# One encoder layer on one core: the order of its stages changed, and seven-product multiplication used for 102 pairs of tiles instead of 81

## The chip, the core and the metric

The kernel runs on one core of one Trainium2 chip, in one launch. The metric is device time in microseconds (us). Times are the median of three runs of the kernel before, 1941.53 us, between 1939.39 and 1941.59. The profile comes from one further execution, which took 1940.43 us.

## What is computed

One layer of a bidirectional encoder: 256 tokens, width 4096, all in float32. The parts that matter here:

```python
h = rms_norm(x, g_mix)
proj = h @ w_in                                   # 4096 -> 1600 + 2048 + 4 x 2048
c_q, c_kv, k_rope, gate_a, q_b, k_b, v_b, gate_b = split(proj)   # 1024, 512, 64, then 2048 each
# latent heads (16): small projections of the latent columns, then dense softmax attention
q_a = rms_norm(c_q) @ w_uq                        # 1024 -> 16 x (128 + 64), the 64 rotated by position
kv  = rms_norm(c_kv) @ w_ukv                      # 512 -> 16 x (128 + 128)
y_a = rms_norm(attention(q_a, kv, k_rope)) * silu(gate_a)
# dilated heads (16): attention with a distance penalty over three window patterns
y_b = rms_norm(dilated(q_b, k_b, v_b)) * silu(gate_b)
x = x + concat(y_a, y_b) @ w_out                  # 4096 -> 4096
gate = sigmoid(rms_norm(x, g_ple) @ w_ple_gate)   # 4096 -> 4096
out = rms_norm(x + (p @ w_ple) * gate, g_final)
```

## The kernel before

**A product.** Every float32 operand of a large multiplication is cut into a high half (rounded by ACT) and a low half (the remainder, by DVE); `split` does it. `mm` then issues three matmuls: high by high, high by low, low by high. The left operand is the transposed activation, kept as tiles of 128 contraction rows by 256 tokens; the right operand is a weight tile of 128 rows by up to 1024 columns, loaded by DMA on SP's queue into one of four `raw` buffers and cut into halves shortly before its use.

**Steps.** All multiplications by weights are laid out in one list, `steps`, in the order in which TensorE takes them. Two kinds of groups fill the list. A `Chunk` takes up to 512 columns in two PSUM banks, two contraction tiles in one step. A `Block` takes 1024 columns in eight banks: its plain steps multiply one contraction tile with four products (two halves of the tokens by two halves of the columns), twelve matmuls of 512 columns. Its fast steps take a *pair* of contraction tiles as a 2 x 2 by 2 x 2 multiplication with seven products in place of eight. For that they need four differences of weight tiles (`fast_steps`, on DVE) whose high and low halves are made anew, and sums and differences of the left operand, which `add_sums` makes once for a stage and several blocks use. The last products are put together on DVE from the banks M1 to M7, M2, M3, M4 and X, in a `mid` task after the last fast step and a `done` task after the block's last step. `spread(n, lead, trail)` lays n pairs between `lead` and `trail` plain steps.

**Tasks.** What is not a weight multiplication (attention of a head, turning a tile, gating, statistics) is a Python generator. `advance` resumes it when a model of the engines' clocks says that its inputs are due no later than `SOON` = 0.3 us after TensorE is free; what the task then emits stands at this place in the queue of each engine. Before, `advance` runs after each step of the list. Weight tiles are converted ahead of their step (`convert_one`), two to five steps.

**The order before.** With the pairs of each block in brackets:

1. latent columns of `w_in` in four chunks of 400, while x is loaded, turned and squared (`x_bank`, `x_square`);
2. a block of latent gate columns (6);
3. eight times: projections `w_uq` and `w_ukv` of two latent heads, between them 512 gate columns (`ga2`), and the attention of the heads (`attend` with `dil` false); then a last gate chunk `ga3`;
4. blocks for the dilated q, k, v, 1024 columns each, in the order q, k, v, q, k, v (6, 8, 8, 8, 8, 4);
5. dilated gate columns in four chunks of 512, 64 steps, beside the attention of the dilated heads;
6. `w_out` in three blocks (4, 7, 4) and two chunks;
7. `w_ple_gate` in three blocks (6 each) and chunks of 512, 256 and 256 columns, with `w_ple`; then the final norm.

All vector, scalar and matmul instructions are recorded at one line of the helper that meters them, L174 (L176 in the changed kernel), so groups are told apart by tiles. The tile names in the profile are `hi` and `lo` for halves of weights, `raw` for loaded weights, `A`, `B`, `T`, `Q` for the large SBUF buffers, and `m`, `s`, `o`, `t` for PSUM banks.

Of the kernel before, what the change touches and what calls it, by code (L numbers as in the profile page):

```python
# [66 lines left out]
class Clock:  # L67
# [31 lines left out]
    def after(self, ap, engine, wrote):  # L99
        name, lo, hi = self.place(ap)  # L100
        times = [self.base.get(name, 0.0)]
        for m in self.marks.get(name, ()):
            if m[0] < hi and lo < m[1]:
                for who in m[2:3] if wrote else m[2:]:
                    times += [t for e, t in who.items() if e != engine]
        return max(times)
# [12 lines left out]
    def run(self, engine, us, outs, ins, late=0.0):  # L119
        at = self.free[engine]  # L120
        for ap in ins:
            at = max(at, self.after(ap, engine, True))
        for ap in outs:
            at = max(at, self.after(ap, engine, False))
        self.free[engine] = at + us
        if late:
            self.free["dma"] = max(self.free["dma"], at + 2.0) + late
            seen = self.free["dma"]
        else:
            seen = at + us + self.SEEN[engine]  # L130
# [65 lines left out]
class Chunk:  # L196
# [4 lines left out]
    def __init__(self, src, nk, n, lhs, banks, done, needs=lambda j: (), per=2, ts=(0, 1), keep=None):  # L201
        self.src, self.nk, self.n, self.lhs, self.banks = src, nk, n, lhs, banks
        self.done, self.needs, self.per, self.ts, self.keep = done, needs, per, ts, keep
        self.ps, self.ring = None, WP
# [3 lines left out]
def encoder_layer(ctx: ExitStack, tc: tile.TileContext, x, p, positions, g_mix, w_in, g_q_latent, w_uq,  # L208
# [61 lines left out]
    nc.gpsimd.dma_start(gains[:32, 0, :], g_mix[0].rearrange("(k p) -> k p", p=P))  # L270
# [37 lines left out]
    def rotary_tables():  # L308
# [26 lines left out]
        nc.scalar.activation(ss[:, :, :half], ss[:, :, half:], AF.Copy, scale=-1.0)  # L335

# [89 lines left out]
    def advance(force=False, spare=True):  # L426
# [21 lines left out]

    def load_x(i):
        xs[i] = slot(f"T{i % 4}", [NT, 512])  # L450
        for o in (0, 256) if i == 0 else (0,):
            n = 256 if i == 0 else 512
# [11 lines left out]
    def x_square(b):  # L464

        i, o = divmod(b, 2)
        if o:
            nc.scalar.activation(xjunk[:, 0], xs[i][:, o], AF.Square, accum_out=sq[:, o, i:i + 1])
        else:
            nc.vector.scalar_tensor_tensor(xjunk[:, 1], xs[i][:, o], 1.0, xs[i][:, o], op0=ALU.mult, op1=ALU.mult,  # L470
                                           accum_out=sq[:, o, i:i + 1])

    def x_bank(b):
# [5 lines left out]
        x_square(b)  # L479

    rx, rxq, rxh = stat(NT), stat(NT), stat(NT)

    def x_stats():
# [4 lines left out]
        nc.vector.tensor_scalar(rxh, rx, 0.5, None, op0=ALU.mult)  # L488

# [4 lines left out]
    c_tok = []  # L494
# [5 lines left out]

    def turn_c(bs):

        for b in bs:
            tag = yield from turned()
            tp = bank(tag, [2, S])
            for k in range(2):
                for t in range(NT):
                    nc.tensor.transpose(tp[:, k, t * P:(t + 1) * P], c_tok[t][:, (2 * b + k) * P:(2 * b + k + 1) * P],
                                        ident)
            yield  # L510
            key, o = ("q", 2 * b) if b < 4 else ("kv", 2 * b - 8)
            split_rows(*(q[:, o:o + 2] for q in cT[key]), tp, G[key][:, o:o + 2])
            give(tag)
            yield

    def done_a(i):
        def task(ps):
            if i == 0:
                yield from x_stats()
                for t in range(NT):  # L520
                    c_tok.append(slot(f"B{t}", [OFF_GA]))
                qh, ql = slot("B4", [8, S], F32R), slot("B5", [8, S], F32R)
                kv = slot("B6", [2, 4, S], F32R)
                cT["q"], cT["kv"] = (qh, ql), (kv[:, 0], kv[:, 1])
            for t in range(NT):
                dst = c_tok[t][:, 400 * i:400 * (i + 1)]
                if t:
                    nc.vector.tensor_scalar(dst, ps[t], rx[:, t:t + 1], None, op0=ALU.mult)
                else:
                    nc.scalar.activation(dst, ps[t], AF.Copy, scale=rx[:, t:t + 1])  # L530
            give(*ps.tags)
            yield
            if i == 3:
                spawn(latents())
            ends = [400 * i, min(400 * (i + 1), Q_LORA + KV_LORA)]
            if ends[0] < Q_LORA < ends[1]:
                ends.insert(1, Q_LORA)
            for lo, hi in zip(ends, ends[1:]):
                c = 4 if lo == Q_LORA else 5 if lo > Q_LORA else i
                for t in range(NT):  # L540
                    nc.scalar.activation(junk[:, :hi - lo], c_tok[t][:, lo:hi], AF.Square,
                                         accum_out=sums[:, c, t:t + 1])
                    yield
            while i and ("cT", i - 1) not in flags:
                yield
            yield from turn_c(((0,), (1, 2), (3,), (4, 5))[i])
            flags.add(("cT", i))
            if i == 3:
                tot = stat(2 * NT).rearrange("p (a t) -> p a t", a=2)
                nc.vector.tensor_tensor(tot[:, 0], sums[:, 0], sums[:, 1], op=ALU.add)  # L550
                nc.vector.tensor_tensor(tot[:, 0], tot[:, 0], sums[:, 2], op=ALU.add)
                nc.vector.tensor_tensor(tot[:, 1], sums[:, 4], sums[:, 5], op=ALU.add)
                yield from rsqrt_mean(rq, tot[:, 0], Q_LORA)
                nc.vector.tensor_scalar(rqs, rq, (NOPE + ROPE) ** -0.5, None, op0=ALU.mult)
                yield from rsqrt_mean(rkv, tot[:, 1], KV_LORA)
                flags.add("latents")
        return task

    def latents():
        kpe = slot("T6", [2, NT, 2, ROPE])  # L560
        for t in range(NT):
            for d in range(2):
                nc.gpsimd.tensor_copy(kpe[:, 1, t, d], c_tok[t][:, Q_LORA + KV_LORA:OFF_GA])
        rk = slot("T5", [NT, 2, ROPE])
        rotate(rk, kpe[:, 1], kpe[:, 0], 2)
        pe = slot("T7", [4, S], F32R)
        T7["pe"] = pe
        yield
        tag = yield from turned()
        tp = bank(tag, [2, S])  # L570
        for t in range(NT):
            nc.tensor.transpose(tp[:, 0, t * P:(t + 1) * P], rk[:, t].rearrange("p d r -> p (d r)"), ident)
        yield
        split(pe[:, 0], pe[:, 1], tp[:, 0])
        give(tag)
        flags.add("kpe")
# [3 lines left out]
    E = {}  # L580

    def attend(h, q_src, k_src, pe, v, y, dil):
# [18 lines left out]
        at_s, at_o = ("m0", "m1") if dil else ("s", "o")  # L601
# [86 lines left out]
    def done_uq(i):  # L688
        def task(ps):
            q = slot("T5", [NT, 2, NOPE + ROPE])  # L690
            kq = slot("T6", [1024])
# [16 lines left out]
            while i and not all(("scored", 0, 2 * i - 1 - n) in flags for n in range(2)):  # L708
                yield
            pe = slot("Q0", [2, S], F32R)  # L710
# [7 lines left out]
    def done_uk(i):  # L718
        def task(ps):
            if i == 0:  # L720
                E["t"] = slot("T4", [2, NT, S])
                E["s"] = stat(2 * 3 * NT).rearrange("p (i a t) -> p i a t", i=2, a=3)
                for j in range(2):
                    ya[j] = slot(f"B{2 + j}", [8, S])
            pr = pairs[i]
            k = pr["kq"][:, :512].rearrange("p (t h d) -> p t h d", t=NT, h=2)
            v = slot(f"B{i % 2}", [2, NT, 2, HD], F32R)
# [1074 lines left out]
```

## Time and profile before

| | before |
|---|---|
| median of 3 runs | 1941.53 us (1939.39 to 1941.59) |
| profiled execution | 1940.43 us, span 1938.7 us |
| TensorE busy, matmuls | 1914.6 us (99%), 9290 |
| weight loads | 1630.6 us (84%) |
| VectorE busy | 1540.0 us (79%) |
| ScalarE busy | 1093.8 us (56%) |
| DMA | 370.59 MB, mean 191 GB/s |

The page gives busy time by engine, the span in 40 slices, the DMA queues, the chain of work that ended last and the costliest groups of instructions. In a row of a group stand the instruction with its output and inputs, shapes and count, then busy time and mean duration of one in ns, then the idle time of the engine before these instructions and what ended it. In the table of stretches each row has the window in us, then for each engine the busy time and, in brackets, the number of instructions.

### The profile page before, as it was taken

Reading aid. Unit: us, or ns where it says so; the run is one execution under the profiler, and the core shown is the slowest. Engines: PE = TensorE matmul, PEld = TensorE weight load, DVE = VectorE, ACT = ScalarE, POOL = GpSimd, SP = SyncE. Lnnn points to the kernel's source line nnn. Section 1 sums busy time; section 2 is a strip of 40 time slices with the busy share of each in tenths; the row PEclk is TensorE's granted clock in tenths of the full one; section 3 lists DMA queues with packets and bytes.
Section 4 is the critical chain, followed back from the end, with each engine's and each line's share of the span. In section 5 each row is a group of like instructions: output and inputs, shape, how many; then the busy total and the mean of one; then the engine's idle time right before and its main releaser. Section 6 shows DMA issues by size and latency. Waiting matters only on the chain.

```text
span 1938.7 us, 25562 instructions
## 1 busy us (share of the span) xinstructions
PE 1914.6 (99%) x9290; PEld 1630.6 (84%) x9290; DVE 1540.0 (79%) x2131; ACT 1093.8 (56%) x1500; POOL 81.2 (4%) x124
## 2 busy tenths in 40 slices
PE   9999999999999999999999999999999999999997
PEld 8998889887788888888888888788888888888887
DVE  7846966666999999999677778889976688889765
ACT  6644555655565565656446666555654456555543
POOL 1001012220000000000000110000000000000000
PEclk9999999999999999999999999999999999999998
DMA  7666644445666666666754456665666656666665
GB/s 252 195 189 194 199 147 152 140 148 159 185 200 207 211 201 196 211 203 207 218 176 142 141 163 194 229 212 182 215 196 202 187 184 215 196 215 194 230 183 176
DMA packets 146478, 370.59 MB, mean 191 GB/s; under 512 B 11924, under 2 KB 45808, under 8 KB 146096
## 3 DMA queue, kind: packets, MB, share of 16 engines
q1 hardware_dynamic: 144432, 361.80, 60.7%
q0 software_dynamic: 1920, 7.15, 1.1%
q8 instruction: 73, 1.20, 0.2%
q14 instruction: 53, 0.43, 0.1%
HBM read 364.72 MB, written 4.19 MB: 190 GB/s over the span
## 4 chain that ended last, share of the span: by engine, by line
PE 89%; DVE 6%; DMA 2%; ACT 2%; issue 1%; DVEq 0%; ACTq 0%; POOLq 0%
PE m L174 51%; PE t L174 17%; PE s L174 11%; PE o L174 10%; DVE lo L174 2%; DVE B L174 1%; DVE T L174 1%; DMA raw<-in_w_ple_gate_dram 1%; ACT hi L174 1%; DMA raw<-in_w_out_dram 1%; DVE Al L174 1%; DMA raw_e<-in_w_ple_dram 0%; DVE st L174 0%; DVE Ah L174 0%; ACT B L174 0%
## 5 line engine op out<-in xcount | busy, mean ns | idle before, releaser
L174 DVE TENSOR_TENSOR lo<-raw,hi 128x1024 fp32r<-128x1024 f32 (+4 forms) x501 | 559.1, 1125 | 240.8 <-ACT hi L174 239.9
L174 ACT ACTIVATE hi<-raw 128x1024 fp32r<-128x1024 f32 (+4 forms) x501 | 488.6, 981 | 423.4 <-PE m L174 146.8
L174 PE MATMUL m<-hi,Ah 128*128 128x512 f32 (+2 forms) x711 | 265.3, 373 | 1.8 <-DVE B L174 1.0
L174 PE MATMUL m<-hi,B 128*128 128x512 f32 (+1 forms) x838 | 265.6, 376 | 0.1
L174 PE MATMUL m<-hi,Al 128*128 128x512 f32 (+2 forms) x717 | 264.0, 368 | 0.0
L174 PE MATMUL m<-lo,Ah 128*128 128x512 f32 (+2 forms) x708 | 261.3, 369 | 1.3 <-DVE lo L174 1.3
L174 DVE TENSOR_TENSOR B<-raw,B 128x1024 fp32r<-128x1024 f32 (+2 forms) x238 | 210.8, 911 | 21.0 <-ACT B L174 18.5
L174 ACT ACTIVATE B<-raw 128x1024 fp32r<-128x1024 f32 (+1 forms) x126 | 121.4, 970 | 99.8 <-PE m L174 24.9
L174 PEld LDWEIGHTS m<-hi,B 128*128 128x128 f32 x838 | 156.0, 188 | 22.6 <-DVE B L174 0.5
L174 PE MATMUL m<-lo,B 128*128 128x512 f32 (+1 forms) x419 | 157.2, 375 | 3.8 <-DVE lo L174 3.8
L174 PEld LDWEIGHTS m<-hi,Ah 128*128 128x128 f32 x711 | 134.2, 189 | 20.1 <-issue 1.7
L174 PEld LDWEIGHTS m<-hi,Al 128*128 128x128 f32 x717 | 135.1, 188 | 18.2 <-DVE Al L174 0.2
L174 PEld LDWEIGHTS m<-lo,Ah 128*128 128x128 f32 x708 | 133.5, 189 | 19.6 <-DVE lo L174 3.0
L174 PE MATMUL m<-B,Ah 128*128 128x512 f32 (+1 forms) x440 | 127.9, 375 | 0.8 <-DVE B L174 0.8
L174 PE MATMUL t<-hi,Al 128*128 128x512 f32 x250 | 97.2, 390 | 0.0
L174 PE MATMUL t<-hi,Ah 128*128 128x512 f32 x246 | 97.1, 395 | 0.0
L174 ACT ACTIVATE hi<-B 128x1024 fp32r<-128x1024 f32 x74 | 77.6, 1059 | 30.3 <-PE t L174 9.8
L174 PEld LDWEIGHTS m<-B,Ah 128*128 128x128 f32 x440 | 80.4, 188 | 16.1 <-DVE B L174 0.9
L174 PE MATMUL t<-lo,Ah 128*128 128x512 f32 x240 | 93.6, 390 | 0.0
L174 PEld LDWEIGHTS m<-lo,B 128*128 128x128 f32 x419 | 78.8, 188 | 17.6 <-DVE lo L174 6.9
L174 DVE TENSOR_TENSOR lo<-B,hi 128x1024 fp32r<-128x1024 f32 x74 | 88.4, 1219 | 5.6 <-ACT hi L174 4.9
L174 PE MATMUL m<-B,Al 128*128 128x512 f32 (+1 forms) x220 | 82.2, 374 | 0.0
(488 smaller groups left out, 3679.1 us busy)
## 6 DMA issues: line engine op xcount, KB each, us to landing
raw<-in_w_in_dram SPq DMA_DIRECT2D x320, 512.0 KB, 4.2
raw<-in_w_out_dram SPq DMA_DIRECT2D x128, 512.0 KB, 4.5
raw<-in_w_ple_gate_dram SPq DMA_DIRECT2D x128, 512.0 KB, 4.6
raw<-in_w_in_dram SPq DMA_DIRECT2D x63, 400.0 KB, 3.5
raw<-in_w_uq_dram SPq DMA_DIRECT2D x32, 384.0 KB, 3.4
raw<-in_w_ukv_dram SPq DMA_DIRECT2D x16, 512.0 KB, 5.0
T<-in_x_dram SPq DMA_DIRECT2D x7, 512.0 KB, 5.8
T<-in_x_dram POOLq DMA_DIRECT2D x7, 512.0 KB, 5.9
```

Source lines behind the costliest of these rows:

```text
L174: return do(out, *rest, **named)
```

## The change

The list of steps is laid out in another order, again with the pairs of each block:

1. the six q, k, v blocks first (3, 7, 7, 8, 8, 6); the first of them begins with contraction tiles 16 to 31, since x now arrives in that order, and one product order differs in its first step;
2. latent columns in chunks of 384, 384, 384 and 448, beside the attention of the dilated heads;
3. all gate columns as four blocks, dilated then latent (5, 7, 7, 7);
4. `w_uq` and `w_ukv` of the eight pairs of latent heads with no other columns between them, uq in banks m0 and m1, ukv in m2 and m3;
5. `w_out` with the rows of the dilated heads first: for columns 3072 to 4095 as two half chunks (`half_o` adds them to the residual), then three blocks over all rows (6, 6, 4), then the other half chunks;
6. `w_ple_gate` in three blocks (7 each) and the same last chunks.

That is 102 pairs. Buffers are given out anew to fit. `advance` is now also called after every product (`tick`), with a second condition, `room() > ROOM`, for resuming a task. The clock model keeps one DMA queue per issuing engine and orders reads and writes of one engine differently. Some tasks change the engine or the order of an operation: `x_square` squares on ACT alone, `done_a` squares out of PSUM, `done_uk` interleaves its two token tiles, and the last stage reads half of the embedding product out of PSUM instead of a copy.

```diff
-        self.free = dict.fromkeys([*self.SEEN, "dma"], 0.0)
+        self.free = dict.fromkeys(self.SEEN, 0.0)
...
-                if due.get(task, 0.0) <= clock.free["pe"] + SOON and (spare or force or task not in lazy):
+                if due.get(task, 0.0) <= clock.free["pe"] + SOON and (force or (spare or task not in lazy) and room() > ROOM):
                     resume(pool, task)
...
+    X_ORDER = 4, 5, 6, 7, 0, 1, 2, 3
...
-        if o:
-            nc.scalar.activation(xjunk[:, 0], xs[i][:, o], AF.Square, accum_out=sq[:, o, i:i + 1])
-        else:
-            nc.vector.scalar_tensor_tensor(xjunk[:, 1], xs[i][:, o], 1.0, xs[i][:, o], op0=ALU.mult, op1=ALU.mult,
-                                           accum_out=sq[:, o, i:i + 1])
+        nc.scalar.activation(xjunk[:, o], xs[i][:, o], AF.Square, accum_out=sq[:, o, i:i + 1])
...
+    C_COLS = (0, 384), (384, 384), (768, 384), (1152, 448)
...
             self.left[m] -= 1
             mm(self.ps[m], a, b, first, self.left[m] == 0)
+            tick()
...
+            more = [*needs, *self.turn_needs]
...
-                self.step("M5 M7", None, lambda hi, lo: split(hi, lo, T[0]), run(("M5", S(0)), ("M7", S(2))), needs, 0, 1.37),
-                self.step("M6 M4", None, lambda hi, lo: split(hi, lo, T[1]), run(("M6", S(1)), ("M4", A22)), needs, 0, 1.37),
+                self.step("M5 M7", None, lambda hi, lo: split(hi, lo, T[0]), run(("M5", S(0)), ("M7", S(2))), more, 0, 1.37),
+                self.step("M6 M4", None, lambda hi, lo: split(hi, lo, T[1]), run(("M6", S(1)), ("M4", A22)), more, 0, 1.37),
...
-    FAST, WIDE = 6, 3
+    FAST, WIDE = 7, 3
...
+    FAST_QKV, LEAD_QKV = (3, 7, 7, 8, 8, 6), (18, 4, 4, 4, 4, 8)
+    FAST_G, LEAD_G = (5, 7, 7, 7), (12, 6, 6, 4)
+    FAST_O, LEAD_O = (6, 6, 4), (4, 5, 4)
...
+    for i, (lo, n) in enumerate(C_COLS):
+        add(Chunk(cols(w_in, lo, n), 32, n, lhs_x, (("m2", "m3"), ("m0", "m1"))[i % 2], done_a(i)))
...
+    for n, (dil, half) in enumerate(((1, 0), (1, 1), (0, 0), (0, 1))):
+        hook(len(steps), only(*(("t0", "t1"), ("m2", "m3"))[n % 2]))
+        order = spread(FAST_G[n], LEAD_G[n], 4)
...
+        blk.turn_needs = ["latents", *(("gated", 1, c) for c in range(min(4, 2 * n)))]
...
+    for i in range(8):
+        for ch in (Chunk(cols(w_uq, 384 * i, 384), 8, 384, lhs_c("q"), ("m0", "m1"), done_uq(i), lambda j: ["latents"]),
+                   Chunk(cols(w_ukv, 512 * i, 512), 4, 512, lhs_c("kv"), ("m2", "m3"), done_uk(i),
...
+    def room():
+
+        c, now = converted[0], ran[0] + 1
+        if c >= len(steps):
+            return 1e9
+        need = max(clock.free["pe"], step_end[0]) + sum(steps[k].time for k in range(now + 1, c))
+        return need - max(clock.free[e] for e in ("dve", "act", "pe"))
+
+    def tick():
+
+        advance(spare=slack(ran[0] + 1) > MARGIN)
```

More of the change, by code (lines that the diff above doesn't have):

```diff
@@ L512, in turn_c @@
-            split_rows(*(q[:, o:o + 2] for q in cT[key]), tp, G[key][:, o:o + 2])
+            split(pe[:, 0], pe[:, 1], tp[:, 0])
             give(tag)
[L514 to L556, printed above, removed]
-        return task
@@ L559, in latents @@
[L559 to L576, printed above, removed]
+            flags.add("latents")
@@ L1521, in encoder_layer @@
[L1521 to L1534 removed]
+            opening = blk
@@ L1629, in split @@
                 return
-            r = raw.pop(i)
-            for k in range(ch.per) if i == 0 else (slice(None),):
-                if i == 0:
-                    split(*lhs_x(k), first[k], G["mix"][:, k:k + 1])
-                split(hi[:, k], lo[:, k], r[:, k])
+            split(hi, lo, raw.pop(i))
             if ch.keep:
```

515 lines of the change are left out of this document (291 added, 224 removed).

## The prediction

> **What bounds the kernel now.** I read the page first, then the table of stretches, then PE's waits, then the groups by shape, last single instructions in time order.
>
> ```profile
> span 1938.7 us, 25562 instructions
> PE 1914.6 (99%) x9290; PEld 1630.6 (84%) x9290; DVE 1540.0 (79%) x2131; ACT 1093.8 (56%) x1500; POOL 81.2 (4%) x124
> PEclk9999999999999999999999999999999999999998
> PE 89%; DVE 6%; DMA 2%; ACT 2%; issue 1%; DVEq 0%; ACTq 0%; POOLq 0%
> ```
>
> TensorE holds 99% of the span and 89% of the chain that ended last, at full clock. VectorE is next at 79%. A busy PE row is modelled, so the rate of issue has to confirm it:
>
> ```profile
> 100.00:150.00 50.00, 50.00 (x280) 49.95 (x279) 24.25 (x26) 22.36 (x34) 0.00 (x0) 1.00 0.70 191
> 300.00:350.00 50.00, 49.33 (x286) 44.53 (x285) 31.61 (x48) 28.96 (x56) 10.77 (x18) 1.00 0.46 142
> 550.00:600.00 50.00, 50.00 (x223) 41.39 (x222) 48.67 (x58) 28.16 (x30) 0.00 (x0) 1.00 0.67 219
> 700.00:750.00 50.00, 50.00 (x222) 41.41 (x221) 48.85 (x56) 30.23 (x32) 0.00 (x0) 1.00 0.69 221
> 850.00:900.00 50.00, 50.00 (x222) 41.42 (x221) 49.33 (x59) 31.47 (x34) 0.00 (x0) 1.00 0.67 206
> 1050.00:1100.00 50.00, 50.00 (x271) 42.73 (x270) 41.67 (x73) 37.59 (x72) 5.85 (x5) 1.00 0.50 146
> ```
>
> The columns are PE, weight loads, DVE, ACT, POOL with their counts, clock, DMA share and GB/s. In stages of 512-column matmuls 222 go through in every 50 us, 0.2252 us each, whatever the other engines do; with 400 columns it is 50/280 = 0.1786 us. The same 222 at three places says that these stages are PE's own pace. The row of 850 us also says that DVE may be busy for 49.33 of 50 us without one lost matmul. What PE waits for by name is little, and half of it lies in the stage of the latent heads (250 to 500 us):
>
> ```profile
> PE m L174 <- DVE lo L174: 5.1, 13, 0.8
> PE m L174 <- DVE B L174: 1.8, 4, 0.7
> PE m L174 <- DVE junk L174: 1.5, 1, 1.5
> PE t L174 <- DVE B L174: 1.1, 1, 1.1
> ...
> PE m L174 <- DVE lo L174: 3.1, 8, 0.8
> PE t L174 <- DVE B L174: 1.1, 1, 1.1
> PE m L174 <- DVE B L174: 0.7, 1, 0.7
> ```
>
> The first four rows are the whole span, the last three the window 250 to 500 us: 4.9 us there. The kernel is bound by the number of matmuls; what can spoil a cut in that number is a DVE without room, or heads whose steps PE has to wait for.
>
> A rule of the Trainium skill (Perfetto Trace Analysis, Identifying the Most-Contended Engine) would have headroom read from the share of weight loads, not of matmuls. By the 84% above TensorE would have a sixth to spare, and fewer matmuls would bring less than their count. The trace does not bear that out: in the rows with 222 matmuls the loads are busy 41.4 of 50 us too, and no matmul is lost there.
>
> **The change part by part.** *Fewer products.* A pair of contraction tiles multiplied in the seven-product form needs seven products instead of eight, and a product is three matmuls of 512 columns. 21 pairs more are 63 matmuls fewer; the order of the two programs' instructions agrees (6762 matmuls of 512 columns before, 6699 after). All pairs lie in the stages of 0.2252 us: 63 x 0.2252 = **-14.2 us**.
>
> The latent columns are cut as 384, 384, 384 and 448 instead of four times 400:
>
> ```profile
> 297.19 0.51 PE L174 MATMUL m<-hi,B 128*128 128x384 f32 x2
> 297.54 0.33 PE L174 MATMUL m<-lo,B 128*128 128x384 f32 x1
> 297.71 0.51 PE L174 MATMUL m<-hi,B 128*128 128x384 f32 x2
> ```
>
> Three of 384 columns take 297.71 - 297.19 = 0.52 us, 0.173 each; 448 lie between 0.1786 and 0.2252, 0.199. Before: 768 x 0.1786 = 137.2 us; after: 576 x 0.173 + 192 x 0.199 = 137.9. No difference beyond the rounding: **0**. Transposes and attention matmuls keep their counts.
>
> A second rule speaks against part of this. The Trainium skill (TensorE: Matmul & The Clock Gate, Back-to-back issue gap) gives about 131 ns for a sustained matmul of 512 columns. By it 63 would bring 8.3 us only. Here a sustained one takes 225 ns in every such stretch.
>
> *What a pair costs DVE and ACT.*
>
> ```profile
> L174 DVE TENSOR_TENSOR lo<-raw,hi 128x1024 fp32r<-128x1024 f32 x365 | 443.8, 1224 | 199.1 <-ACT hi L174 198.2
> L174 DVE TENSOR_TENSOR lo<-B,hi 128x1024 fp32r<-128x1024 f32 x74 | 88.4, 1219 | 5.6 <-ACT hi L174 4.9
> L174 DVE TENSOR_TENSOR B<-raw,B 128x512 f32<-128x512 f32 x112 | 77.0, 688 | 1.9
> L174 DVE TENSOR_TENSOR lo<-raw,hi 128x512 fp32r<-128x512 f32 x51 | 34.9, 683 | 1.2 <-ACT hi L174 1.2
> L174 DVE TENSOR_TENSOR T<-T 128x128 f32<-128x128 f32 x56 | 13.8, 288 | 1.0
> L174 DVE SCALAR_TENSOR_TENSOR Al<-t,gT,Ah 128x256 fp32r<-128x256 f32 x52 | 22.8, 478 | 7.2 <-ACT Ah L174 7.2
> L174 DVE SCALAR_TENSOR_TENSOR B<-m,st,B 128x512 f32<-128x512 f32 x23 | 15.9, 743 | 0.1
> L174 ACT ACTIVATE hi<-raw 128x1024 fp32r<-128x1024 f32 x365 | 385.0, 1060 | 352.8 <-PE m L174 111.2 <-PE t L174 66.2 <-PE o L174 57.7
> L174 ACT ACTIVATE hi<-raw 128x512 fp32r<-128x512 f32 x51 | 32.0, 628 | 32.1 <-PE t L174 12.8 <-issue 8.9 <-PE m L174 3.4
> ```
>
> Two plain steps: 2 x 1.224 = 2.45 us of DVE. A pair: four differences of 512 columns (4 x 0.688), a low half of 512 (0.683), one of 1024 (1.224) and two of differences (2 x 1.219): 7.10 us. So 4.65 us more, x 21 = 98 us, and DVE goes from 1540 to some 1638 us, 85% of the new span. ACT: 0.628 + 3 x 1.060 against 2 x 1.060, 1.69 x 21 = 35 us; 59%. The sums of the left operands stay at 28 (6+8+8+6 before; 8+7+6+7 after). None of this is on PE's path as long as a block has room. A gate block with 7 pairs: PE 32 x 12 x 0.2252 - 7 x 0.676 = 81.8 us. DVE: 18 x 1.224 + 7 x 7.10 = 71.7, and for gating 12 operations of 512 columns (0.68) and 8 of 256 (0.48), 12.0, together 83.7 us of durations. Durations overlap at their ends, so I scale by a block that is in the trace: a key block with 8 pairs has 16 x 1.224 + 8 x 7.10 + 7 x 0.74 = 81.6 us of them in 81.1 us of PE, and its stretch (550 to 600) shows 48.67 of 50, or 0.967 of their sum. So a gate block fills DVE to 83.7 x 0.967 / 81.8 = 98.9%, just what the row of 850 us bore without loss. The first 150 us are as crowded: x is still being turned (32 pieces of 0.48 us), eight sums at 0.68 + 4 x 0.288 + 0.68 = 2.5 us are made, and blocks of 7 pairs follow at once. Bounds 0 and +8 (below, the second rival), taken **+1**, near the 0 because the rows from 550 to 900 are the nearest.
>
> *Latent heads alone.* Today each pair of heads hides its hand-offs under its projections and under 24 matmuls of gate columns (5.4 us); the gate columns go. What must be hidden, from one head of the trace:
>
> ```profile
> 318.55 0.60 PE L174 MATMUL t<-ident,T 128*128 128x128 f32 x4
> 319.32 0.60 ACT L174 ACTIVATE T<-t 128x512 fp32r<-128x512 f32 x1
> 319.95 0.69 DVE L174 TENSOR_TENSOR T<-t,T 128x512 fp32r<-128x512 f32 x1
> ...
> 297.56 0.68 DVE L174 TENSOR_REDUCE st<-s 128x2 f32<-128x512 f32 x1
> 298.28 0.47 ACT L174 ACTIVATE T<-s,st 128x256 f32<-128x256 f32 x1 [1.89 <-DVE st L174]
> 299.54 0.62 DVE L174 TENSOR_SCALAR T<-T,st 128x256 f32<-128x256 f32 x2
> ```
>
> From the last transpose to usable halves: 320.64 - 318.98 = 1.7 us (four transposes issue 0.108 apart). From scores to scaled weights: 300.16 - 297.56 = 2.6, with its hand-offs 2.9. A head has 1.7 + 2.9 + 1.7 = 6.3 us of hand-offs, a pair 12.6, and a pair's own projections are 48 x 0.173 + 24 x 0.2252 = 13.7 us. It fits, with little over. In the order of the changed program the work put between a head's transposes and its scores is 1.6 to 5 us (before: 2.1 and 7.5), between scores and weights' transposes 4.8 to 8.0 except for the last two heads with 2.5 and 3.4 (before: 5.4 and 9.8), between those and the output 1.4 to 5.2 (before: 5.2 to 5.9). So most hand-offs are still covered and some eight are at their limit. The planner puts a piece in PE's queue up to SOON = 0.3 us before its data is due. It did so between steps; now it does so after every product, three matmuls or 0.5 to 0.7 us, so a piece is more often early. Bounds: 48 hand-offs x 0.3 = +14.4 above; -4.9 below, if the waits of 250 to 500 us have no successor. Taken: half of 0.3 on each, 7.2, less the 4.9 that are waited for today: **+2.3**.
>
> *Dilated heads beside latent columns.* The cover of 64 steps falls from 64 x 12 x 0.2252 = 173 to 64 x 12 x 0.18 = 138 us, and sixteen heads at the spacing of 5.4 and 8.1 us take 108. The stretch of 1050 us, heads beside wider columns, has no lost matmul and DVE at 41.67 of 50. A narrower step also has a narrower conversion, so DVE's share rises by the heads alone. Bounds 0 and 48 hand-offs at a third of SOON, +5; taken **+0.5**.
>
> *Gates as blocks, the split output projection, the start, the end.* A new wait: a block's steps for M5, M7, M6 and M4 stand behind the transposes of the gate before it, which stand behind DVE and ACT work of its last sums. Behind them in PE's queue is everything. Cover: 4 to 12 plain steps of 12 x 0.2252 = 2.7 us, 11 to 32 us, against four sums, four tanh, four products and two scalings at 0.6 to 0.7, some 10 us. Nothing, but it is near at 4 steps; +1 to +2 if it is late. The latent gates have the two half chunks of dilated rows, 2 x 16 x 6 x 0.2252 = 43 us, for y's statistics and multiplication; the four additions of 0.68 that half_o brings and the residual's DMAs on POOL's queue lie there too: nothing. At the start the first weight tile comes as one 512 KB piece, a small DMA stands ahead of x on SP's queue instead of POOL's, and squares move from DVE to ACT: -1 to +2, taken 0. The end is the same code: the last matmul is issued at 1925.50 of 1938.7 us and what follows keeps its 13.2 us.
>
> ```profile
> 1925.50 0.28 PE L174 MATMUL m<-hi,Al 128*128 128x256 f32 x1
> ```
>
> **Sum.** -14.2 + 0 + 1 + 2.3 + 0.5 = -10.4 us. The profiled execution took 1940.43 us (1.7 around its span), inside the range of the three runs, 1939.39 to 1941.59, and 1.1 under their median: 1930.0 us on its footing, 1931.1 on the median's. I keep the first, **1930**, since the runs spread as far.
>
> **The rivals.** *The new order also loses today's waits.* PE's named waits, 9.5 us in the rows above of which 1.5 are the start, come from hand-offs fixed at step ends; finer placing could remove the 4.9 us of the latent heads and add none: 1940.4 - 14.2 - 4.9 = 1921. For: the waits recur with every pair of heads. Against: less cover.
>
> *DVE becomes the bound in crowded blocks.* If the durations do not overlap more than PE allows, three gate blocks lose 83.7 - 81.8 = 1.9 us each, three last blocks with 7 pairs (71.7 + 16 x 0.68 = 82.6) 0.8 each: +8 in place of the +1, so 1930 + 7 = 1937. For: 98.9%. Against: the row of 850 us.
>
> *Latent heads exposed, and slower than before.* Without the gate columns each pair loses 5.4 us of cover. Where half of it was needed, PE waits 2.7 us per pair, eight times, 21.6 us: 1940.4 - 14.2 + 21.6 = 1948. It decides from (14.2 + 3.9) / 8 = 2.3 us per pair on. For: distances of 1.4 to 2.1 us against hand-offs of 1.7. Against: 12.6 us of hand-offs in 13.7 us of projections, and DVE and ACT at 31.61 and 28.96 of 50 in today's stage.
>
> *A matmul removed frees less than its spacing.* If the weight load sets the pace, it frees 41.42 / 221 = 0.187 us: 63 x 0.187 = 11.8, 1940.4 - 11.8 + 3.8 = 1932. The second rule above would go further in this direction. Against: the loads leave 8.6 of 50 us free where nothing else waits.
>
> That the pairs are not made is excluded by the 63 missing matmuls.
>
> **How the numbers follow.** My sum and what lies around it (1924 to 1935) gets 0.55, the lost waits 0.15, DVE as bound 0.16, exposed heads 0.12, the cheaper matmul 0.02. What three runs can tell from no change is about 0.2%, 3.9 us: faster is under 1937.6. That holds the sum, the lost waits, the cheaper matmul and half of DVE's case: 0.80. The other half of it lies within 0.2%: 0.07, with 0.01 beyond. Slower: 0.13. The range takes in the lost waits and DVE's case and leaves out the exposed heads and a little below: 1920 to 1941.
>
> **What would show it.** Right: 63 matmuls fewer at 222 per 50 us in all blocks; PE's named waits 11 to 16 us in all; DVE near 1640 us; a stage of latent heads of about 8 x 19.5 = 156 us plus a few. Wrong: fewer than 222 in the gate blocks with waits for DVE lo (second rival), 22 us or more from one pair's first projection to the next one's (third), a clock row under 9 after the start, or a tail over 14 us.

## The result, and the profile after

| | before | after |
|---|---|---|
| median (runs) | 1939.92 us (6; 1939.02 to 1941.59) | 1932.98 us (6; 1930.70 to 1935.15) |
| profiled execution, span | 1940.43, 1938.7 us | 1933.49, 1931.7 us |

The six runs before are the three of the forecast and three more. The ratio is 0.9963, with a 95% interval from 0.9951 to 0.9976: about 7 us faster. The forecast was 10.4 us off the profiled execution, 1930.0; its range of 1920 to 1941 holds the result.

The page of the changed kernel, its span, engines, clock and chain:

```profile
span 1931.7 us, 25573 instructions
PE 1902.9 (99%) x9227; PEld 1614.5 (84%) x9227; DVE 1639.1 (85%) x2270; ACT 1130.2 (59%) x1556; POOL 75.2 (4%) x123
PEclk9999999999999999999999999999999999999999
PE 80%; DVE 11%; issue 3%; ACT 3%; DMA 2%; POOL 1%; SPq 0%; DVEq 0%; ACTq 0%; POOLq 0%
```

63 matmuls are gone, and DVE has gained 99 us, to 1639.1. The share of DVE on the chain has risen from 6% to 11%: more of what ends last is now a vector operation. Where that costs time is not on the page. The table of stretches has it (columns: window, PE, weight loads, DVE, ACT, POOL with counts, clock, DMA share, GB/s):

```profile
100.00:150.00 50.00, 47.48 (x202) 38.81 (x201) 49.52 (x73) 26.97 (x34) 0.00 (x0) 0.97 0.62 200
300.00:350.00 50.00, 50.00 (x222) 41.40 (x222) 46.95 (x55) 31.56 (x33) 0.00 (x0) 1.00 0.68 211
900.00:950.00 50.00, 50.00 (x222) 41.18 (x221) 47.61 (x55) 31.24 (x32) 0.00 (x0) 1.00 0.65 203
1050.00:1100.00 50.00, 47.86 (x297) 43.90 (x296) 39.58 (x62) 32.14 (x71) 13.66 (x21) 1.00 0.45 135
```

The q, k, v blocks (300) and the gate blocks (900) still pass 222 matmuls in 50 us, with DVE at 47 and 48 of 50. Matmuls are missing in two places: 20 of them around 100 us, under a clock of 0.97, and in the latent heads from 1050 us on. PE's waits, the larger of them (us in total, times, longest):

```profile
PE t L176 <- ACT Al L176: 3.7, 5, 1.0
PE o L176 <- DVE B L176: 2.5, 1, 2.5
PE m L176 <- DVE lo L176: 2.2, 3, 1.2
PE t L176 <- DVE T L176: 1.9, 3, 1.3
PE m L176 <- DVE junk L176: 1.5, 1, 1.5
```

The first two rows were not there before. They are the two places: one wait of 2.5 us at the second block, and five waits in the latent heads for ACT's rounding of a rotated tile.

For a balance I took from both traces the distances between the starts of successive matmuls. The median distance of each width is its pace (512 columns 227 ns, 448 203, 400 180, 384 174, 256 120, a transpose 108). What a distance has beyond its pace is lost time, summed here by stage:

| term | forecast | measured |
|---|---|---|
| matmuls at their pace (1901.0 to 1887.9 us) | -14.2 | -13.1 |
| opening and blocks (3.8 to 8.1 up to 250 us; gate and q, k, v blocks after that 0 both times) | +1 | +4.3 |
| latent heads (10.7 to 12.8) | +2.3 | +2.1 |
| dilated heads, latent columns (1.5 to 2.7) | +0.5 | +1.2 |
| output projection to the last matmul (7.3 to 6.5) | 0 | -0.8 |
| after the last matmul's start (13.2 to 12.5) | 0 | -0.7 |
| sum | -10.4 | -7.0 |

The spans differ by the same 7.0 us. Of the opening's 8.1 us, 4.3 lie between 100 and 200 us (0.5 before) and 3.5 in the first 50 (2.8 before).

### The profile page after: what moved, and what is told of

Its sections match the earlier page's. It is cut to its first block, busy times and chain, and to the rows that moved or that the text cites. A ratio compares the mean times of both kernels' runs of the same rounds, so it can differ in the third digit from the quotient of the medians.

```text
span 1931.7 us, 25573 instructions
## 1 busy us (share of the span) xinstructions
PE 1902.9 (99%) x9227; PEld 1614.5 (84%) x9227; DVE 1639.1 (85%) x2270; ACT 1130.2 (59%) x1556; POOL 75.2 (4%) x123
## 3 DMA queue, kind: packets, MB, share of 16 engines
q8 instruction: 72, 1.18, 0.3%
## 4 chain that ended last, share of the span: by engine, by line
PE 80%; DVE 11%; issue 3%; ACT 3%; DMA 2%; POOL 1%; SPq 0%; DVEq 0%; ACTq 0%; POOLq 0%
PE m L176 44%; PE t L176 17%; PE s L176 10%; PE o L176 9%; DVE B L176 4%; DVE lo L176 3%; DVE T L176 1%; DVE Al L176 1%; ACT hi L176 1%; POOL Al L176 1%; DMA raw<-in_w_ple_gate_dram 1%; DMA raw<-in_w_in_dram 1%; DVE Ah L176 1%; ACT T L176 1%; DVE st L176 1%
## 5 line engine op out<-in xcount | busy, mean ns | idle before, releaser
L176 ACT ACTIVATE hi<-raw 128x1024 fp32r<-128x1024 f32 (+3 forms) x486 | 467.4, 969 | 347.0 <-PE m L176 107.8
L176 DVE TENSOR_TENSOR lo<-raw,hi 128x1024 fp32r<-128x1024 f32 (+3 forms) x486 | 537.9, 1115 | 137.2 <-ACT hi L176 133.8
L176 PE MATMUL m<-hi,Ah 128*128 128x512 f32 (+3 forms) x815 | 298.2, 380 | 0.9 <-ACT hi L176 0.9
L176 PE MATMUL m<-hi,Al 128*128 128x512 f32 (+3 forms) x807 | 289.7, 371 | 0.0
L176 PE MATMUL m<-hi,B 128*128 128x512 f32 (+2 forms) x772 | 244.7, 371 | 0.8 <-ACT Ah L176 0.4
L176 DVE TENSOR_TENSOR B<-raw,B 128x1024 fp32r<-128x1024 f32 (+2 forms) x209 | 189.0, 913 | 15.1 <-ACT B L176 13.2
L176 PE MATMUL m<-lo,B 128*128 128x512 f32 (+2 forms) x386 | 142.2, 368 | 1.2 <-DVE lo L176 1.2
L176 DVE TENSOR_TENSOR T<-t,T 128x512 fp32r<-128x512 f32 (+2 forms) x73 | 49.8, 685 | 41.3 <-ACT T L176 40.9
L176 PE MATMUL t<-hi,Ah 128*128 128x512 f32 (+1 forms) x226 | 84.4, 388 | 0.0
L176 DVE TENSOR_TENSOR T<-raw,T 128x512 f32<-128x512 f32 (+2 forms) x101 | 77.6, 777 | 3.9 <-ACT T L176 2.5
L176 PE MATMUL t<-lo,Ah 128*128 128x512 f32 (+1 forms) x185 | 72.1, 390 | 0.0
```

What stands on the lines that cost most here:

```text
L176: return do(out, *rest, **named)
```

## The experiments

Three questions: what makes the opening lose 4.3 us more than before, what makes the latent heads lose 12.8, and what a pair is worth where DVE is nearly full. In what follows "loss" is time beyond the pace as above, from the one profiled execution of a kernel; for the changed kernel it is 29.9 us in all.

**The wait of 2.5 us at the second block.** In the changed kernel the second block's first step writes bank o, which the first block's last additions must have emptied. Timeline, PE and DVE (start, duration, engine, output and inputs):

```profile
102.51 0.39 PE L176 MATMUL s<-hi,Al 128*128 128x512 f32 x1
105.42 0.50 PE L176 MATMUL o<-hi,Ah 128*128 128x512 f32 x1 [2.52 <-DVE B L176]
...
106.88 0.63 PE L176 MATMUL t<-hi,Al 128*128 128x512 f32 x1
107.31 0.63 PE L176 MATMUL t<-hi,Ah 128*128 128x512 f32 x1
...
95.90 2.03 DVE L176 SCALAR_TENSOR_TENSOR T<-T 128x64 f32<-128x64 f32 x8
97.85 2.35 DVE L176 TENSOR_TENSOR lo<-raw,hi 128x1024 fp32r<-128x1024 f32 x2
...
101.86 2.19 DVE L176 SCALAR_TENSOR_TENSOR B<-t,st,B 128x512 f32<-128x512 f32 x3
103.96 1.40 DVE L176 SCALAR_TENSOR_TENSOR B<-o,st,B 128x512 f32<-128x512 f32 x2
```

The additions from bank o end at 105.36 and PE goes on at 105.42. Ahead of them on DVE stand eight small operations of the rotary tables (2.03 us) and conversions. From 106.45 us on, eight matmuls come 427 ns apart (106.88 to 107.31 is 0.43), not 227: another 1.6 us. First, the rotary tables later:

```diff
-    hook(24, lambda: spawn(rotary_tables()))
+    hook(150, lambda: spawn(rotary_tables()))
```

> The rotary tables, some 20 small DVE operations that the changed kernel makes near 83 to 98 us, are made from step 150 on instead of step 24. Theory (DVE backlog in the opening): PE's wait of 2.5 us for DVE B near 102 us shrinks by the 2 to 3 us of small operations, the half-clock matmuls behind it (8 x 0.2 = 1.6 us) go too, -3 to -4.3 us, about 1929 us. Rival (the bank would be late anyway, its sums stand behind weight halves): under 1 us of change.

1932.0 us (1931.52 to 1933.0), ratio 0.9959 [0.9946, 0.9971]. The wait is 1.6 instead of 2.5 us and none of the following matmuls is slow; the loss from 100 to 200 us falls from 4.3 to 1.7. The median falls by only 1 us, less than expected. In the profile the whole loss falls by 2.0 (29.9 to 27.9), since the stretch from 1200 to 1300 us loses 1.2 more than in the changed kernel (3.0 to 4.2). The rest is not explained; the six runs of the changed kernel have clocks of 0.996 to 0.998 and spread by 4.5 us, the five here have 0.998 and spread by 1.5, so the medians may not compare like with like. Next, more plain steps between the first block's last pair and its end:

```diff
-        order = spread(FAST_QKV[n], LEAD_QKV[n], (2, 2, 2, 2, 2, 5)[n])
+        order = spread(FAST_QKV[n], LEAD_QKV[n], (6, 2, 2, 2, 2, 5)[n])
```

> The first block ends on six plain steps instead of two after its last pair; its three pairs stay. The sums that free bank o then have 16 us of matmuls to hide under instead of 5. Theory (DVE backlog at the hand-over of the bank): the wait of 2.5 us near 102 us goes, -4 us, about 1929 us. Rival (DVE is short of time over the whole first 150 us): the wait moves to a later step as a wait for DVE lo or DVE B, change under 1 us.

1939.02 us, ratio 0.9997 [0.9988, 1.0006]: the whole gain gone. The wait grew to 3.7 us, and waits for DVE's B (1.5) and lo (0.8) appeared ahead of it. The edit also moves the pairs closer together and earlier, and the first 100 us lose 8.5 instead of 3.9. More distance for the hand-over did not help, which speaks for a lack of DVE's time there. One pair fewer in the first block:

```diff
-    FAST_QKV, LEAD_QKV = (3, 7, 7, 8, 8, 6), (18, 4, 4, 4, 4, 8)
+    FAST_QKV, LEAD_QKV = (2, 7, 7, 8, 8, 6), (18, 4, 4, 4, 4, 8)
```

> The first block gets 2 pairs instead of 3: 3 matmuls of 512 columns more, +0.7 us, and 4.65 us less for DVE before 100 us. Theory (DVE has too much to do in the first 100 us): the wait of 2.5 us for DVE B near 102 us and the half-clock matmuls behind it go, -2.7 to -4.3, together -2 to -3.6, 1929 to 1931 us. Rival (the wait has another cause, such as the loading of x): the wait stays and the time rises by 0.7.

1933.26 us, ratio 0.9966 [0.9953, 0.9978], no difference from the changed kernel. At the place itself the theory holds in part: a wait of 1.9 us remains, no slow matmul follows it, and the loss from 100 to 200 us falls from 4.3 to 2.1. But three matmuls more are issued, and in this execution the first 50 us lose 5.4 instead of 3.5, as the clock is halved from 13.56 to 16.97 us. Last, the product that needs bank o placed at the end of the step:

```diff
-                order = ("M2", 0, 0), ("X", 1, 1), ("M3", 0, 1), ("M4", 1, 0)
-                if first_:
-                    order = order[0], order[3], order[1], order[2]
+                order = ("M2", 0, 0), ("M3", 0, 1), ("M4", 1, 0), ("X", 1, 1)
+                if first_:
+                    order = order[0], order[2], order[3], order[1]
```

> Plain steps of a block issue their products in the order M2, M3, M4, X in place of M2, X, M3, M4, so that bank o (product X), which the first block's last additions free, is needed six matmuls, some 1.36 us, later. Nothing else changes. Theory (the second block's first step waits for bank o, 2.5 to 2.7 us at 102.5 us, and this pause sometimes costs half the clock for eight matmuls): the wait falls to about 1.3 us, the half clock goes, the loss in 100 to 200 us falls from 4.4 to about 2, median about 1931. Rival (bank o is only the last of several banks that stand behind the same DVE queue): the wait goes over to M3's bank and nothing changes, 1933.

1932.33 us, ratio 0.9958 [0.9944, 0.9971]. The wait splits into 0.42 (bank t) and 0.35 us (bank o), no slow matmul, loss from 100 to 200 us 1.9. Theory and rival each had a part: the other bank did become a wait, but a small one. From 1200 to 1300 us the loss rose by 2.4 us (3.0 to 5.4), so the median moved by 0.6 only. Why stays open; with all three edits (below) the same stretch loses 1.9.

**The latent heads.** One rotation on POOL in the changed kernel, timeline around 1060 us:

```profile
1058.86 0.95 DVE L176 TENSOR_TENSOR Ah<-raw,Ah 128x768 fp32r<-128x768 f32 x1
...
1060.07 0.46 POOL L176 TENSOR_TENSOR Al<-Ah,cc 128x128 f32<-128x128 f32 x1 [6.78 <-ACT Ah L176]
1060.48 1.05 POOL L176 TENSOR_TENSOR Al<-Ah,ss 128x64 f32<-128x64 f32 x2
...
1061.28 1.07 DVE L176 TENSOR_TENSOR Al<-raw,Al 128x768 fp32r<-128x768 f32 x1
1061.50 1.18 POOL L176 TENSOR_TENSOR Al<-Ah,cc 128x128 f32<-128x128 f32 x1
...
1062.64 1.05 POOL L176 TENSOR_TENSOR Al<-Ah,ss 128x64 f32<-128x64 f32 x2
1063.77 0.72 POOL L176 TENSOR_TENSOR Al<-Al 128x256 f32<-128x256 f32 x1
1063.87 1.44 DVE L176 TENSOR_TENSOR lo<-raw,hi 128x768 fp32r<-128x768 f32 x1
1064.53 0.42 ACT L176 ACTIVATE Al<-Al 128x256 f32<-128x256 f32 x1 [1.60 <-POOL Al L176]
...
1065.00 0.65 PE L176 MATMUL t<-ident,Al 128*128 128x128 f32 x4 [0.98 <-ACT Al L176]
```

The same operation on cc takes 0.46 us once and 1.18 the other time, when a DVE operation with two inputs is under way; DVE's lo of 768 columns takes 1.44 beside POOL's addition (the operation of 768 columns at 1058.86, with POOL idle, took 0.95). From 1060.07 to 1064.49 the rotation takes 4.4 us; over the eight pairs it takes 3.5 to 5.1. The planner prices the seven operations at 0.0024 us per column plus 0.1, together 2.5. So it queues PE's transposes too early, and here PE waits 0.98 us. In the kernel before, the rotations took as long (3.8 to 4.9 us) and PE had no wait for them: under the gate columns the wrong price did not matter. The 2.5 us "on POOL alone" of the first expectation below is that price and no measured time; the shortest rows of the seven add up to 2.8 us (2 x 0.46, 2 x 0.60, 0.72). The Trainium skill (SBUF — State Buffer, SBUF: two separate sides) has a rule for this: GpSimd and VectorE share a pair of ports, which one instruction holds for its whole length, and a vector operation with two SBUF inputs needs it. The row agrees: POOL's operation of 1061.50 ends at 1062.68, 0.33 after DVE's ends at 1062.35, and 0.46 alone is near that.

Three ways to test it. Rotate on DVE:

```diff
-            nc.gpsimd.tensor_tensor(dst[:, t], src[:, t], c, op=ALU.mult)
+            nc.vector.tensor_tensor(dst[:, t], src[:, t], c, op=ALU.mult)
...
-        nc.gpsimd.tensor_tensor(dst, dst, tmp, op=ALU.add)
+        nc.vector.tensor_tensor(dst, dst, tmp, op=ALU.add)
```

> The seven operations that rotate a pair of latent heads (and the shared rotary key) run on DVE instead of POOL. In the changed kernel they take 2.5 us on POOL alone and up to 4.4 us where DVE works at the same time, and PE waits five times for what follows them, 3.7 us. Theory (POOL's chain is what heads without cover expose): these waits go, 2 to 5 us less, 1928 to 1931 us. Rival (heads simply have too little cover): the waits turn into waits for DVE T or lo in the same stage, no change within 1 us, or slower since DVE gets 14 us more to do.

1931.37 us, ratio 0.9957 [0.9945, 0.997], not to be told from the changed kernel. The waits for ACT's Al fall from 3.7 to 0.2 us, as POOL's theory has it, and the eight pairs with the 35 us behind them lose 10.5 us instead of 12.7. But others come elsewhere (DVE T 2.6, DVE B 1.6, ACT hi 2.0), and the loss is 31.1 us in all, in an execution that was the slowest of the five and had three stretches at half the clock. The early placing itself, which my forecast blamed:

```diff
-    SOON = 0.3
+    SOON = 0.0
```

> The planner resumes a task only when its data is due, not up to 0.3 us before (SOON 0 instead of 0.3). The term of the forecast: half of 0.3 us on each of 48 hand-offs is 7 us, so -7 us, about 1926. Rival (the waits of the latent heads come from chains that the planner prices too low, above all POOL's): within 2 us of the changed kernel, with the same waits for ACT Al.

1935.56 us, ratio 0.9981 [0.9972, 0.999]: slower than the changed kernel by 2.6 us in the medians, 3.5 by the ratios. In the heads themselves the edit helps: the waits on Al fall to 2.0, and the eight pairs with the 35 us behind them lose 10.5 us instead of 12.7. But at 809 us, in a gate block, a wait of 3.0 us for DVE's B comes in with slow matmuls behind it; from 800 to 1000 us 6.2 us are lost, where the changed kernel loses none. So being early costs some 2 us in the heads, and over the whole kernel it is worth more than that. And the price alone, with POOL left at its work:

```diff
-                us = n * 0.0024 + 0.1
+                us = n * 0.0024 + 0.4
```

> The planner's price of a POOL operation is raised by 0.3 us, to what one takes beside a busy DVE (4.6 us for the seven of a rotation instead of 2.5); the instructions stay the same and only their order moves. If the waits for ACT Al come from the wrong price alone, they go and 3 to 4 us with them, about 1929. If the stage has too little to put in between, they come back as other waits in the same stage, as when the rotation ran on DVE: within 2 us of the changed kernel.

1928.05 us (1927.69 to 1928.77), ratio 0.9941 [0.9927, 0.9954], the best of the single edits, some 4 to 5 us under the changed kernel. PE's waits from 1040 to 1250 us:

```profile
PE t L176 <- ACT Al L176: 1.0, 1, 1.0
PE t L176 <- DVE T L176: 0.5, 2, 0.3
PE m L176 <- ACT Ah L176: 0.4, 1, 0.4
PE o L176 <- DVE T L176: 0.3, 1, 0.3
```

Al has fallen from 3.7 to 1.0, the loss of the eight pairs and the 35 us behind them from 12.7 to about 9 us, the whole loss from 29.9 to 25.2. POOL's rotations take about as long as before (3.2 to 5.1 us); only the plan knows it now.

**Is it cover?** My third rival had the heads exposed because no other columns stand between them. First try: the eight steps of one half chunk of `w_out` between the projections of the last four pairs. To free banks for it, both projections of a pair went to m2 and m3:

```diff
-        for ch in (Chunk(cols(w_uq, 384 * i, 384), 8, 384, lhs_c("q"), ("m0", "m1"), done_uq(i), lambda j: ["latents"]),
+        for ch in (Chunk(cols(w_uq, 384 * i, 384), 8, 384, lhs_c("q"), ("m2", "m3"), done_uq(i), lambda j: ["latents"]),
...
+            if i > 3:
+                k = 2 * (i - 4) + (ch.nk == 4)
+                add(cover, k, k + 1)
```

> Cover is given back to the last four pairs of latent heads alone: the eight steps of the first half chunk of w_out (dilated rows) stand between their projections, one behind each, and for that both projections of a pair share banks m2 and m3 (in all eight pairs). No multiplication is added or taken. Cover theory (heads wait because no other columns stand between them): the loss of about 12 us in the latent heads falls most in pairs 4 to 7, to about 8 in all, 1929. Rival (the waits are set by a late POOL chain that the planner prices too low, and are not shortened by cover, since the planner puts the piece as early as its model allows in any case): the waits on ACT Al stay near 3.7 us, the loss stays at 11 to 13, 1933 or, from the shared banks, up to 1936.

1972.98 us, ratio 1.0166 [1.0153, 1.018]: 40 us slower, which neither theory expected. Two things were changed at once, so the banks alone came next (the first two lines of the diff, nothing else):

> Only one edit: w_uq's products use banks m2 and m3 like w_ukv's, for all eight pairs of latent heads; no half chunk is moved. If the 40 us that the kernel with the moved half chunk lost come from the shared banks, this one loses what that one lost before 1140 us in the pairs without cover (some 18 us more than in the changed kernel) and about as much in the later pairs: 1955 to 1970. If they come from the half chunk that is missing behind the heads, this one stays within 5 us of 1933 there and only the first pair, whose banks the gate transposes use too, costs some 10: 1940 to 1945.

1961.76 us, ratio 1.0108 [1.0091, 1.0125]. The shared banks alone cost 29 us. Its waits from 1040 to 1140 us:

```profile
PE m L176 <- ACT Ah L176: 8.8, 4, 5.7
PE m L176 <- DVE B L176: 6.6, 4, 2.3
PE t L176 <- ACT Al L176: 1.9, 3, 1.0
```

The next projection now waits until ACT and DVE have emptied the banks of the one before. The loss by pair, from the first projection of one to that of the next:

| pair | 0 | 1 | 2 | 3 | 4 | 5 | 6 | 7 | 35 us after |
|---|---|---|---|---|---|---|---|---|---|
| changed kernel | 0.6 | 2.5 | 1.3 | 1.1 | 1.7 | 1.5 | 0.8 | 1.7 | 1.5 |
| shared banks | 9.9 | 5.9 | 4.2 | 4.2 | 4.2 | 5.1 | 6.7 | 3.4 | 1.1 |
| shared banks, cover in pairs 4 to 7 | 9.9 | 6.0 | 4.2 | 4.2 | 1.0 | 1.9 | 3.3 | 3.6 | 6.2 |

With shared banks cover does count: it takes the pairs 4 to 6 from 16.0 to 6.2 us. Behind the heads, where the half chunk is then missing, more is lost than that: 19.9 us in the 105 us after the last pair, against 1.7. So with two banks and no cover a pair is exposed, at 3.4 to 6.7 us each after the first; with four banks, as in the changed kernel, it loses 1.4 on average. The kernel before had both projections of a pair on m2 and m3, with the gate columns as cover on m0 and m1. The change thus gave two more banks to the projections when it took the cover away. Whether cover would still bring something with four banks was not run.

**What a pair is worth, and what holds it up.** The three crowded gate blocks with 3 pairs instead of 7:

```diff
-    FAST_G, LEAD_G = (5, 7, 7, 7), (12, 6, 6, 4)
+    FAST_G, LEAD_G = (5, 3, 3, 3), (12, 6, 6, 4)
```

> Three of the four gate blocks get 3 pairs instead of 7: 12 pairs fewer, 36 matmuls of 512 columns more, and 56 us less for DVE there. If a matmul costs its spacing of 0.2265 us: +8.2 us, about 1941. If it costs its weight load alone, 0.187: +6.7, about 1940. If DVE were the bound of these blocks: 0 to +3, about 1933 to 1936.

1940.69 us, ratio 1.0004 [0.9995, 1.0013]. 36 matmuls more cost 7.7 us, 0.21 each. With the spread of the runs this time alone does not tell the two expectations of 8.2 and 6.7 us apart. The rate does: between 800 and 1000 us DVE falls from 44 to 48 busy us of 50 to 34 to 36, and the matmuls stay at 222 (once 223 or 230) per 50 us with seven pairs as with three, so one more costs its spacing. DVE falls to 1586.8 us in all, and that brings nothing: the gate blocks were not bound by it. Then the finer placing taken out, so that tasks are resumed after a step only:

```diff
     def tick():

-        advance(spare=slack(ran[0] + 1) > MARGIN)
+        return
```

> Tasks are resumed after each step again, not after each product; the order of the stages and the 102 pairs stay. Theory (the finer placement is what lets the heads run with so little cover): the stage of the latent heads, which waits 12 us in the changed kernel, waits far more, over 15 us on top, so 1945 us or more, slower than the kernel before. Rival (the finer placement is what made the new waits): 3 to 7 us faster than the changed kernel, 1926 to 1930.

2074.89 us, ratio 1.0698 [1.0682, 1.0715], with as many matmuls. Rows of its table of stretches, dilated heads and a q, k, v block:

```profile
700.00:800.00 100.00, 73.49 (x390) 60.02 (x390) 75.55 (x202) 60.41 (x136) 15.81 (x25) 0.88 0.17 48
300.00:350.00 50.00, 50.00 (x222) 41.44 (x221) 47.83 (x57) 31.89 (x33) 0.00 (x0) 1.00 0.65 201
```

PE stands idle for a quarter of 700 to 800 us, and the clock falls to 0.88 with it; the block without heads runs as before. The losses sum to 168 us, of which 65 between 600 and 800 and 52 between 1200 and 1400. The new order of stages stands on the finer placing.

**Three edits together.** POOL's price, the rotary tables later, and bank o last:

> Three edits together: the planner's price of a POOL operation 0.0024 us per column plus 0.4 instead of 0.1, the rotary tables 126 steps later (hook 150 instead of 24), and the order M2, M3, M4, X in plain steps. If the causes are separate places (latent heads: some 4 to 5 us; the second block's first step: 1 to 3 us) the gains add: 1924.5 to 1927, PE loss beyond the pace about 22 us, no half clock at 100 us. If they share the slack of the same DVE queue, the time stays at that of the POOL price alone, 1928.

1925.04 us (1924.4 to 1926.15), ratio 0.9921 [0.9907, 0.9934]: faster than the kernel before by 15 us and than the changed one by about 8. Its first waits and its stretch from 100 us:

```profile
PE m L176 <- DVE lo L176: 2.3, 4, 1.1
PE t L176 <- DVE T L176: 1.8, 3, 1.2
PE m L176 <- DVE junk L176: 1.5, 1, 1.5
PE m L176 <- ACT hi L176: 1.3, 2, 0.7
PE t L176 <- ACT Al L176: 1.0, 1, 1.0
...
100.00:150.00 50.00, 49.80 (x219) 40.77 (x218) 49.62 (x71) 25.75 (x30) 0.00 (x0) 1.00 0.64 206
```

219 matmuls where there were 202, at full clock, with DVE as full as before. The loss is 22.5 us against 29.9. The two places, heads and second block, were separate, and their gains add up. At the second block the two edits overlap: alone they took 2.6 and 2.4 us off the 4.3 between 100 and 200 us, together 3.8.

## Why the prediction was right, point by point

*Fewer products, -14.2.* Right: the sum of the paces fell by 13.1. 63 x 0.227 = 14.3 (the forecast's 0.2252 is a little low, since a stretch also counts matmuls that reach over its edges); the latent columns gave back 1.0 (768 x 0.180 = 138.2 before, 576 x 0.174 + 192 x 0.203 = 139.2 after), where I had 0.7 and called it 0; the other 0.2 is the distance behind two single small matmuls, which has no median. The fourth rival, 0.187 per matmul, falls by the rate: the row of 900 us has 222 in 50 us, with seven pairs as with three.

*DVE and ACT.* Right: DVE 1639.1 us (forecast 1638), ACT 59%. The gate blocks fill DVE for 44 to 48 of 50 us, not for the 98.9% that I had reckoned, and lose nothing; from the output projection to the last matmul no more is lost than before. So the second rival, DVE as bound in the gate and last blocks, did not come about.

*The opening, +1.* The term that was mis-sized: 4.3, inside its bounds of 0 and 8, and the largest part of the 3.4 us that the forecast was off. I took the value near 0 because the rows from 550 to 900 us were the nearest. In them, too, DVE's additions empty the banks of one block for the next, and PE does not wait; but there DVE has little else to do than conversions and these additions. With x's turning, sums and rotary tables on DVE as well, a hand-over came 2.5 us late. I had no step for the hand-over of banks between blocks, and none for the clock that falls after it.

*Latent heads, +2.3.* The size was right, 2.1, and that is luck: the mechanism was right in small part only. I charged half of SOON on each hand-off, 7.2 us; without SOON the heads lose 2.2 us less, not 7.2, and the kernel is slower. I took off 4.9 for waits that would go; the named waits from 1040 to 1250 us are 5.9. The larger cause was POOL's rotation, priced at 2.5 us and taking 3.5 to 5.1: with a higher price the heads lose almost 4 us less. The third rival, exposed heads, did not happen, and the shared banks show from what it was saved: four banks, of which my argument on cover did not speak. The sign I gave for it was a bad one: pairs 2 and 3 are 23.4 and 22.1 us from the next one's first projection, over my 22, with a loss of 1.3 and 1.1 only, presumably because the planner moves pieces of heads from one pair to the next. The mean of the first seven is 20.3.

*The first rival, lost waits.* Half true: the waits for `lo` did go (5.1 to 2.2 us), and others of the same size took their place. PE's named waits are 16 us in all, the upper edge of my 11 to 16.

*Dilated heads, +0.5; start and end, 0.* The heads cost 1.2, as much as a single wait of 1.3 us of transposes for DVE's T. The start is in the opening's 4.3. What follows the last matmul's start became 0.7 shorter, 1919.19 to 1931.7; I had taken it for the same code, though the change touches the last stage: DVE's last operation ends 2.7 us after the final scaling begins, where it was 3.4.

## What to carry to other kernels

When an engine beside the bound is at 95%, ask for each buffer that is handed over which operation empties it and what stands ahead of that in the same queue; the rate of conversions does not show it. A planner's price for an operation should be the one under contention, from a trace of the stage it runs in: 0.3 us per POOL operation in the model brought more than moving the work. And dependent stages can be carried by cover or by more banks: with two banks a pair of heads lost 3.4 to 6.7 us without cover, while the whole stage lost 10.7 us with two banks and gate columns, and 12.8 with four banks and nothing between.

## What the runs showed of the hardware

*A short pause can cost clock, and where it falls decides.* Seven profiled executions have the pause of 2.9 us between two matmuls' starts at 102 to 103 us. In five of them (the changed kernel, rotation on DVE, no SOON, POOL's price, shared banks) 5 to 8 of the matmuls that followed came 427 ns apart and the granted clock from 100 to 150 us was 0.97; in two (fewer gate pairs, cover moved) none did, at 1.00. With waits of 1.6 and 1.9 us at this place none did; with 3.7 us eight did. A wait of 1.6 us can suffice elsewhere: with the rotation on DVE such matmuls follow one at 732 us. Stretches of 3.41 us around the pause, the changed kernel first, then the one with the cover moved:

```profile
103.01:106.43 3.42, 1.01 (x4) 0.86 (x5) 3.38 (x6) 1.40 (x2) 0.00 (x0) 1.00 0.57 220
106.43:109.84 3.41, 3.41 (x9) 2.65 (x8) 3.24 (x11) 0.00 (x0) 0.00 (x0) 0.50 0.62 159
101.55:104.96 3.41, 1.58 (x7) 0.96 (x6) 3.38 (x6) 1.06 (x1) 0.00 (x0) 1.00 0.95 360
104.96:108.37 3.41, 2.74 (x12) 2.28 (x13) 3.31 (x7) 0.63 (x1) 0.00 (x0) 1.00 0.28 56
```

The half clock lasts from 106.43 to 109.84 us, 3.41 us, and its start is 29 such lengths after the first entry of the trace's clock record, at 7.44 us. In the five executions TensorE was busy, as the profile models it, for 0.89 to 1.36 us of the 3.41 us ahead of the half clock. In the two others, counted in the same way from their own first entry, the pause lies across a border, and TensorE was busy for at least 1.58 us on either side. So where the pause falls in a fixed grid accounts for all seven. A limit does not follow: 1.63 us at 732 us were followed by half clock, 1.56 us in the kernel with two pairs in the first block were not. The Trainium skill (TensorE: Matmul & The Clock Gate, Part 1: The HAM clock gate) tells of a window of 3.4 us that runs free of the kernel, after which an idle TensorE gets half the clock. The stretches of 3.41 us agree with it; 2.9 us sufficed at times, which is shorter than that figure.

*POOL beside DVE.* A POOL operation of 128 columns took 0.46 us in one row and 1.18 in another of the same rotation, and a DVE operation of 768 columns 0.95 with POOL idle and 1.44 beside it. The forecast had no term for POOL, which is busy for 4% of the span.
